# Conv states in three tiles and steps, first unit's weights split earlier, down steps in later slots of a two-layer trunk

## The chip, the cores and the metric

The kernel runs on one NeuronCore of a Trainium2 chip. The metric is the device time of one launch in microseconds. Each engine (TensorE = PE, VectorE = DVE, ScalarE = ACT, GpSimd = POOL, SyncE = SP) has its own instruction queue and works through it in order; one engine waits for another through semaphores only.

## What is computed

One inference step of a two-layer trunk for 512 prompt tokens and 8 samples of 8 tokens, 576 columns in all, with a model width of 1024. Layer 0 mixes with attention and a gated recurrence, layer 1 with a causal pooling; after each mixer follows the gated ConvFFN, which is where the change lies:

```python
def _conv_ffn(xn, prev, w_up, cw, cb, w_down):
    u = jnp.einsum("btd,df->btf", xn, w_up)            # 1024 -> 2 * 3072
    uc, new_prev = _causal_dwconv(u, prev, cw, cb)     # 3 taps; prev: state_ffn_conv of the samples
    g, val = jnp.split(uc, 2, axis=-1)
    return jnp.einsum("btf,fd->btd", jax.nn.gelu(g) * val, w_down), new_prev
```

## The kernel before

**Arithmetic.** Channels lie on the 128 partitions, tokens in the free dimension, in two halves of 288. Every operand of a matmul is split into a high and a low part (ACT rounds: "hi"; DVE subtracts: "lo"), and each product is three matmuls. So each weight block costs an ACT cast and a DVE subtraction (`wform`, lines 1375 and 1376, tiles `whl`), and each activation too (`hh`, `hl`, lines 1276 and 1277).

**The ConvFFN (`ffn`, line 1224 on).** The up projection makes 24 channel blocks of gate and value. The first six pairs go the usual way (`up_pair`, matmuls at line 143). The other 18 pairs go in 18 "units" (`unit`, line 1400): a unit n makes two channel blocks by seven products of 12 matmuls (line 1382), named "1" to "7", on sums and differences of weight quarters (made by POOL, lines 1407 to 1416) and of activations (`sums`, lines 1359 and 1360). Even n are gates, odd n values. At the end of a unit (`p3`) the two blocks go through the convolution (`conv`: POOL lines 1258 to 1260, ACT 1264, DVE 1265 and 1266); after an odd n comes the product of gate and value (`gate`: DVE 1272, 1273, then `hh`, `hl`).

**Down steps.** The down projection of four gated blocks (a group q) into output block m is a down step `(q, m)`: 24 matmuls (`dn_p`, line 1514) into two PSUM banks, one for each half of the columns. DVE then adds the two halves to the residual (`add_x`, line 711, "L711"), and that frees the banks. The pool of banks (tile `mmb`) has three, so the second bank of a down step is the one that the first L711 of the step ahead has freed, or the one of its second L711. The 32 down steps of q = 0 to 3 are put between other products: four in pairs 4 and 5, the other 28 in "slots" of the units: slot A lies between "6" (with "1" of unit n+1) and "7"; slot B lies after "7" and "2", "5" of unit n+1, and ahead of "4" and "3". `plan` (lines 1549 to 1575) lists the products in order. `prepare(j)` issues the weight splits of plan entry j, three entries ahead of its matmuls.

**What sets the order.** The program is written in the order of `plan`, but a scheduler at compile time places the instructions on each engine by their modelled readiness and by priority; `wform` and the evacuations of the products stand in high-priority blocks, the `gate` work and L711 do not. The finished order is fixed, and each engine runs its own part in order.

**Conv states.** The sample's states of the convolution (`state_ffn_conv`) come in 12 pieces (`states(a)`, line 1236): a DMA of 32 KB (line 1238, tile `fst`, two buffers), a PE transpose (line 1240), an ACT copy (line 1241). Two pieces are done in pair 0, the other ten one by one in later pairs as background steps (`self.bg`, run by `tick()`).

**Loads.** One SP queue issues all weight loads: raw weights of the pairs (`wraw`, line 120), quarters of the units (line 1394), down weights (`wd`, line 1504).

Of the kernel before, what the change touches and what calls it, by code (L numbers as in the profile page):

```python
# [8 lines left out]
F32 = mybir.dt.float32  # L9
# [34 lines left out]
class Trunk:  # L44
# [1179 lines left out]
    def ffn(self, l, after, first=0):  # L1224
# [8 lines left out]
        with self.tc.tile_pool(name="ff", bufs=2, reuse_waits="tile") as fp, ExitStack() as side:  # L1233
            stT = fp.tile([P, 48, 16], F32, name="fstT", bufs=1)

            def states(a):
                st = fp.tile([64, P], F32, name="fst", bufs=2)
                nc.sync.dma_start(st, so[:, a * 512:(a + 1) * 512].rearrange("r (j p) -> r j p", p=P))
                tp = self.bank()
                PE.transpose(tp[:, 0:64], st, self.ident[0:64, 0:64])  # L1240
                A.copy(stT[:, a * 4:(a + 1) * 4, :], tp[:, 0:64].rearrange("p (r j) -> p j r", j=4))

            for a in (1, 7, 2, 8, 3, 9, 4, 10, 5, 11):
                self.bg.append(lambda a=a: states(a))
            hs = {}
            uts = {}
            raws = {}
# [32 lines left out]
            def up_pair(i):  # L1280

                if i % 2 == 0:
                    for s in range(2):
                        if i == 0 and self.up0:
                            raws[s] = self.up0[0][s]
                            continue
                        raws[s] = self.raw(up[:, :, s * DFF + i * P:s * DFF + (i + 2) * P], 8, 256)
                pss = []
                for s in range(2):
                    if i == 0 and self.up0:  # L1290
                        hi, lo = self.up0[1][s]
                    else:
                        hi, lo = self.split(raws[s][:, :, i % 2 * P:i % 2 * P + P], 8, P)
                    pss.append(self.mm3(hi, lo, self.xs, 8, first, [self.px.tile([P, 512], F32, name="pu", tag="XY"[s], bufs=2)
                                                                   for _ in range(2)]))
                    if i == 0 and s == l:
                        states(0)
                        states(6)
                    if i:
                        for _ in range(2):  # L1300
                            if todo:
                                todo.popleft()()
                    if i >= 4:
                        down_now()
                if i == 5:
                    while todo:
                        todo.popleft()()
                    sums()
                ts = []
                for s in range(2):  # L1310
                    ps, u = pss[s], new_u(s, i)
                    V.tensor_tensor(u[:, 2:2 + HT], ps[0][:, 0:HT], self.rb[:, 0:HT], MUL)
                    V.tensor_tensor(u[:, 2 + HT:514], ps[1][:, 0:NP - HT], self.rb[:, HT:NP], MUL)
                    V.tensor_tensor(b10(u, 2, 8), b8(ps[1][:, NP - HT:HT]), b8(self.rb[:, NP:T]), MUL)
                    ts.append(conv(u, s, i))
                gate(i, *ts)
# [8 lines left out]
            def normed(fq):  # L1325
                for p in range(2):
                    xa.append(fq.tile([P, 4, HT], F32R, name="xa", tag=f"xa{p}", bufs=1))
                    xb.append(fq.tile([P, 4, T], F32R, name="xb", tag=f"xb{p}", bufs=1))
                for t, n in ((xa, "a0"), (xb, "b0")):
                    X[n] = [v[:, :, 0:HT] for v in t]  # L1330
                X["b1"] = [v[:, :, HT:T] for v in xb]

                def norm(c):
                    for k in (c, c + 4):
                        V.scalar_tensor_tensor(xn[k], self.xT[:, k, :], self.g_ffn(l, k), self.rb, MUL, MUL)

                def parts(c):
                    for x, v in ((xa, xn[c][:, 0:HT]), (xb, xn[c + 4])):
                        A.copy(x[0][:, c, :], v)
                        V.tensor_tensor(x[1][:, c, :], v, x[0][:, c, :].bitcast(F32), SUB)  # L1340

                def mixed(c):
                    a0, a1 = xn[c][:, 0:HT], xn[c][:, HT:T]
                    b0, b1 = xn[c + 4][:, 0:HT], xn[c + 4][:, HT:T]
                    V.tensor_tensor(a0, a1, a0, SUB)
                    V.tensor_tensor(a1, b1, a1, SUB)
                    V.tensor_tensor(b1, b1, a0, SUB)
                    V.tensor_tensor(b0, b0, b1, SUB)

                for c in range(4):  # L1350
                    for f in (norm, parts, mixed):
                        todo.append(lambda f=f, c=c: f(c))

            def sums():
                for h, (n0, n1) in enumerate((("t1", "t3"), ("t4", "t2"))):
                    th, tl = self.half("xh", h), self.half("xl", h)
                    for c in range(4):
                        v = xn[4 * h + c]
                        A.copy(th[:, c, :], v)
                        V.tensor_tensor(tl[:, c, :], v, th[:, c, :].bitcast(F32), SUB)  # L1360
                    X[n0] = [v[:, :, 0:HT] for v in (th, tl)]
                    X[n1] = [v[:, :, HT:T] for v in (th, tl)]

            box = deque()
            turn = [0]

            def wform(v):

# [18 lines left out]
            def load(n, f, h):  # L1387

                if n > 17:
                    return  # L1390
                if n < 2 and n not in rw:
                    rw[n] = self.wr.tile([P, 2048], F32, name="wraw", tag="wraw")
                c0 = n % 2 * DFF + (6 + n // 2 * 2 + f) * P
                nc.sync.dma_start(quarter(n, f, h), up[:, 4 * h:4 * h + 4, c0:c0 + P])
# [5 lines left out]
            def unit(n):  # L1400
# [80 lines left out]
                def p3(w):  # L1481
                    prod(st["Y"], w, X["b1"], False)
                    with self.tc.high_priority():
                        two(st["u"][0], st["Y"], st["c"])
                    ts[s] = [conv(st["u"][f], s, i + f) for f in range(2)]
                    if s:
                        for f in range(2):
                            gate(i + f, ts[0][f], ts[1][f])
                            if (i + f) % 4 == 3:

                                self.bg.extend([lambda: None] * 2)
                                for a in range(2):
                                    self.bg.append(lambda q=(i + f) // 4, a=a: tails(q, a))

# [25 lines left out]
            def tails(q, s):  # L1520
                tp = self.bank()
                PE.transpose(tp[0:72, 0:P], uts[q][:, s].rearrange("p r j -> p (r j)"), self.ident)
                tl = fp.tile([72, P], F32, name="tl", bufs=2)
                A.copy(tl, tp[0:72, 0:P])
                cs = slice(s * DFF + q * 512, s * DFF + (q + 1) * 512)
                nc.sync.dma_start(O["ffn_conv_p"][l, 0, :, cs].rearrange("b (j p) -> b j p", p=P), tl[0:8])
                nc.sync.dma_start(os_[:, cs].rearrange("b (j p) -> b j p", p=P), tl[8:72])
# [5 lines left out]
                dn_p(q, m, dn_w(q, m))  # L1533
                self.tick()

            self.psum(3)
            fq = side.enter_context(self.tc.tile_pool(name="fq", bufs=1, reuse_waits="tile"))
            for i in range(6):
                up_pair(i)
                if i == 0:  # L1540
                    normed(fq)
                if i == 3:
                    for s in range(2):
                        self.bg.append(lambda s=s: tails(0, s))
            for n in range(2):
                for f, h in ((0, 0), (1, 0), (1, 1), (0, 1)):
                    load(n, f, h)

            units = {}
            plan = []  # L1550

            def put(n, names):
                for c in names:
                    plan.append(("up", n, c))

            def put_down():
                plan.append(("down",) + downs.popleft())

            put(0, "12")
            put(1, "1")  # L1560
# [1 line left out]
            for n in range(18):  # L1562
                nx = n + 1 if n < 17 else None
                put(n, "6")
                if nx is not None and n:
                    put(nx, "1")
                if 1 <= n <= 10 or n in (12, 14):
                    put_down()
                put(n, "7")
                if nx is not None:  # L1570
                    put(nx, "25")
                if n < 16:
                    put_down()
                put(n, "43")
            assert not downs

            ready = {}

# [7 lines left out]
                    else:  # L1586
                        ready[j] = dn_w(a, b)

            for j in range(3):
                prepare(j)  # L1590
            for j, (kind, a, b) in enumerate(plan):
                prepare(j + 3)
                if kind == "up":
# [291 lines left out]
```

## Time and profile before

| | |
|---|---|
| time, median of 3 runs | 1267.13 us (1264.13 to 1269.37) |
| the profiled execution | 1277.01 us, its span 1275.3 us |
| PE busy | 1229.1 us, 96% of the span |
| DVE busy | 1001.1 us, 78% |
| ACT busy | 665.3 us, 52% |
| POOL busy | 432.9 us, 34% |

The profiled execution is 9.9 us above the median of the timed runs. PE is the engine to look at: in the 46.2 us in which it is idle another engine decides, and where its granted clock is below 1.00 its matmuls are slower. A row of a timeline gives start, duration, engine, line, operation, and in square brackets the idle time ahead of it on its engine with what ended it.

### The profile page before, as it was taken

Reading aid. Unit: us, or ns where it says so; the run is one execution under the profiler, and the core shown is the slowest. Engines: PE = TensorE matmul, PEld = TensorE weight load, DVE = VectorE, ACT = ScalarE, POOL = GpSimd, SP = SyncE. Lnnn points to the kernel's source line nnn. Section 1 sums busy time; section 2 is a strip of 40 time slices with the busy share of each in tenths; the row PEclk is TensorE's granted clock in tenths of the full one; section 3 lists DMA queues with packets and bytes.
Section 4 is the critical chain, followed back from the end, with each engine's and each line's share of the span. In section 5 each row is a group of like instructions: output and inputs, shape, how many; then the busy total and the mean of one; then the engine's idle time right before and its main releaser. Section 6 shows DMA issues by size and latency. Waiting matters only on the chain. (4 is left out here: it accounts for less than half of the span.)

```text
span 1275.3 us, 23464 instructions
## 1 busy us (share of the span) xinstructions
PE 1229.1 (96%) x8990; PEld 1170.4 (92%) x8990; DVE 1001.1 (78%) x1891; ACT 665.3 (52%) x1277; POOL 432.9 (34%) x674
## 2 busy tenths in 40 slices
PE   8989999999999899999999999999899999999998
PEld 6968887889899899999999999889899999999998
DVE  6827968897898788888878857798878988888941
ACT  6638557774445455455555535444454555555631
POOL 2240044410113444443544642211534434444400
PEclk9989999999999999999999999989999999999999
DMA  5314234323223223223321322322332323232231
GB/s 165 102 36 136 67 113 117 108 70 100 75 86 94 83 84 94 88 89 92 94 67 44 109 64 77 86 76 71 93 92 70 99 86 100 84 94 67 86 95 50
DMA packets 144772, 111.68 MB, mean 88 GB/s; under 512 B 8705, under 2 KB 135817, under 8 KB 144652
## 3 DMA queue, kind: packets, MB, share of 16 engines
q1 hardware_dynamic: 140516, 101.69, 26.1%
q0 software_dynamic: 3072, 8.46, 2.4%
q8 instruction: 71, 1.16, 0.4%
q14 instruction: 41, 0.34, 0.1%
q10 hardware_dynamic: 1072, 0.04, 0.1%
HBM read 104.14 MB, written 6.25 MB: 87 GB/s over the span
## 5 line engine op out<-in xcount | busy, mean ns | idle before, releaser
L1382 PE MATMUL pX<-xh,whl 128*128 128x288 f32 x864 | 192.4, 298 | 6.9 <-ACT c L1467 6.9
L1514 PE MATMUL mmb<-hh,whl 128*128 128x288 f32 x1024 | 190.0, 296 | 4.1 <-DVE xT L711 4.1
L1376 DVE TENSOR_TENSOR whl<-wraw,whl 128x512 fp32r<-128x512 f32 x216 | 155.8, 743 | 25.5 <-ACT whl L1375 23.9
L1514 PEld LDWEIGHTS mmb<-hh,whl 128*128 128x128 f32 x1024 | 154.6, 189 | 4.9 <-DVE xT L711 4.6
L1375 ACT CAST whl<-wraw 128x512 fp32r<-128x512 f32 x216 | 128.2, 620 | 47.5 <-PE mmb L1514 15.7
L1382 PEld LDWEIGHTS pX<-xh,whl 128*128 128x128 f32 x864 | 144.9, 188 | 8.1 <-ACT c L1467 7.4
L143 PE MATMUL pu<-xh,whl 128*128 128x288 f32 x768 | 143.1, 304 | 2.7 <-DVE whl L131 2.0
L1260 POOL COPY ut<-u 128x18 f32<-128x18 f32 x96 | 40.8, 425 | 279.0 <-DVE u L1444 164.7
L711 DVE TENSOR_TENSOR xT<-mmb,xT 128x288 f32<-128x288 f32 x174 | 72.3, 449 | 75.4 <-PE mmb L143 47.2
L1382 PE MATMUL pX<-xl,whl 128*128 128x288 f32 x432 | 127.7, 296 | 0.0
L130 ACT CAST whl<-wraw 128x1024 fp32r<-128x1024 f32 (+1 forms) x68 | 69.5, 1023 | 106.3 <-PE mmb L143 29.8
L143 PEld LDWEIGHTS pu<-xh,whl 128*128 128x128 f32 x768 | 116.7, 193 | 5.1 <-DVE whl L131 2.6
L1514 PE MATMUL mmb<-hl,whl 128*128 128x288 f32 x512 | 111.8, 298 | 5.5 <-DVE hl L1277 5.5
L1265 DVE SCALAR_TENSOR_TENSOR t<-u,par,t 128x592 f32<-128x592 f32 x96 | 96.3, 1007 | 23.7 <-ACT t L1264 23.4
L131 DVE TENSOR_TENSOR whl<-wraw,whl 128x1024 fp32r<-128x1024 f32 (+1 forms) x68 | 83.3, 1227 | 26.8 <-ACT whl L130 21.5
L1264 ACT ACTIVATE t<-u,par 128x592 f32<-128x592 f32 x96 | 84.3, 882 | 36.3 <-DVE u L1444 22.1
L1266 DVE SCALAR_TENSOR_TENSOR t<-u,par,t 128x592 f32<-128x592 f32 x96 | 90.5, 945 | 1.3
L1514 PEld LDWEIGHTS mmb<-hl,whl 128*128 128x128 f32 x512 | 82.7, 189 | 6.9 <-DVE hl L1277 6.9
L143 PE MATMUL pu<-xl,whl 128*128 128x288 f32 x384 | 84.8, 301 | 1.6 <-DVE xl L293 1.6
L1276 ACT CAST hh<-hf 128x576 fp32r<-128x576 f32 x48 | 32.4, 674 | 96.6 <-DVE hf L1273 95.8
L1382 PEld LDWEIGHTS pX<-xl,whl 128*128 128x128 f32 x432 | 81.4, 188 | 0.0
L1407 POOL TENSOR_TENSOR wraw<-wraw 128x512 f32<-128x512 f32 x36 | 58.4, 1623 | 46.4 <-DMA wraw<-in_ffn_w_up 39.8
(453 smaller groups left out, 3118.6 us busy)
## 6 DMA issues: line engine op xcount, KB each, us to landing
wraw<-in_ffn_w_up SPq DMA_DIRECT2D x144, 256.0 KB
wd<-in_ffn_w_down SPq DMA_DIRECT2D x32, 512.0 KB
wraw<-in_ffn_w_up SPq DMA_DIRECT2D x12, 1024.0 KB
wraw<-in_ab_w_in SPq DMA_DIRECT2D x9, 1024.0 KB
wraw<-in_ffn_w_down SPq DMA_DIRECT2D x8, 1024.0 KB
wraw<-in_ab_w_out SPq DMA_DIRECT2D x4, 1024.0 KB
xt<-in_x_prompt SPq DMA_DIRECT2D x4, 512.0 KB
out_y_p<-y SPq DMA_DIRECT2D x8, 256.0 KB
```

The source lines that it names most:

```text
L130: keep(self.nc.scalar.copy(hi, v))
L131: keep(self.nc.vector.tensor_tensor(lo, v, hi.bitcast(F32), SUB))
L143: nc.tensor.matmul(ps[hf][:, 0:HT], w[:, k, :], x[:, hf * HT:(hf + 1) * HT], start=(n == 0 and j == 0), stop=(n == K - 1 and j == 2))
L711: self.nc.vector.tensor_tensor(x, ps[hf][:, 0:HT], x, ADD)
L1264: A.activation(t, u[:, 2:594], AF.Identity, scale=self.fw(l, 2, ch), bias=self.fb(l, ch))
L1265: V.scalar_tensor_tensor(t, u[:, 1:593], self.fw(l, 1, ch), t, MUL, ADD)
L1266: V.scalar_tensor_tensor(t, u[:, 0:592], self.fw(l, 0, ch), t, MUL, ADD)
L1375: A.copy(f[:, 0], v)
L1376: V.tensor_tensor(f[:, 1], v, f[:, 0].bitcast(F32), SUB)
L1382: PE.matmul(ps[:, 0:HT], w[:, a, k, :], x[b][:, k, :], start=(start and k == 0 and j == 0), stop=(k == 3 and j == 2), skip_group_check=True)
L1407: G.tensor_tensor(a21, a11, a21, SUB)
L1514: PE.matmul(ps[hf][:, 0:HT], w[:, a, k, :], hs[4 * q + k][b][:, hf * HT:(hf + 1) * HT], start=(k == 0 and j == 0), stop=(k == 3 and j == 2))
```

## The change

Four edits in `ffn`, the same in both layers:

1. The 12 pieces of the conv states go into three tiles (in the buffers of the tag `hl`) by 12 DMAs at the entry of `ffn`; three steps of four transposes and four copies take the place of twelve steps. The first step runs in pair 0, the others as background steps.
2. The loads of units 0 and 1 and `prepare(0)`, `prepare(1)` move ahead of `sums()` in pair 5, `prepare(2)` behind it; the first `whl` buffer that `wform` takes is another (`turn`).
3. The list of slots: slot A before at n = 1 to 10, 12, 14, now at 1 to 14; slot B before at n = 0 to 15, now at 0 to 15 without 2 and 13. So the group q = 1 starts in slot A of n = 3 instead of slot B of n = 2, q = 2 in slot A of n = 7 instead of slot B of n = 6, q = 3 in slot A of n = 11 instead of slot B of n = 10.
4. `tails` (transposes of the new states, line 1522) come one tick later.

```diff
-            def states(a):
-                st = fp.tile([64, P], F32, name="fst", bufs=2)
-                nc.sync.dma_start(st, so[:, a * 512:(a + 1) * 512].rearrange("r (j p) -> r j p", p=P))
+            sts = []
+            for q in range(3):
+                t = fp.tile([P, T], F32, name="fst", tag="hl", bufs=9)
+                sts.append(t[0:64, 0:512].rearrange("p (a c) -> p a c", a=4))
+                for a in range(4):
+                    c0 = (a % 2 * 6 + 2 * q + a // 2) * 512
+                    nc.sync.dma_start(sts[q][:, a, :], so[:, c0:c0 + 512].rearrange("r (j p) -> r j p", p=P))
+
+            def states(q):
                 tp = self.bank()
-                PE.transpose(tp[:, 0:64], st, self.ident[0:64, 0:64])
...
-            for a in (1, 7, 2, 8, 3, 9, 4, 10, 5, 11):
-                self.bg.append(lambda a=a: states(a))
+                for a in range(4):
+                    PE.transpose(tp[:, a * 64:(a + 1) * 64], sts[q][:, a, :], self.ident[0:64, 0:64])
...
                     while todo:
                         todo.popleft()()
+                    for n in range(2):
+                        for f, h in ((0, 0), (1, 0), (1, 1), (0, 1)):
+                            load(n, f, h)
+                    prepare(0)
+                    prepare(1)
                     sums()
+                    prepare(2)
...
-            turn = [0]
+            turn = [2]
...
-                                self.bg.extend([lambda: None] * 2)
+                                self.bg.extend([lambda: None] * 3)
...
+            later = deque(list(downs)[4:])
...
-                if 1 <= n <= 10 or n in (12, 14):
+                if 1 <= n <= 14:
                     put_down()
                 put(n, "7")
                 if nx is not None:
                     put(nx, "25")
-                if n < 16:
+                if n not in (2, 15, 16, 17) and n != 13 or n == 15:
                     put_down()
                 put(n, "43")
```

The order on DVE in layer 0, unit 4, slot B, in the kernel before. Tiles carry their numbers: `mmb_5812` and `mmb_5813` are the two banks of the down step in slot A of the same unit, `hf`, `hl` belong to the gate of units 2 and 3, `c1` and `pZ` to the next unit's products, `whl_5882` to weights two products on.

```order
L1273 TENSOR_TENSOR hf_5760<-t_5531,t_5748 128x64
L1272 TENSOR_TENSOR hf_5768<-t_5538,t_5755 128x512
L1273 TENSOR_TENSOR hf_5768<-t_5538,t_5755 128x64
L711 TENSOR_TENSOR xT_73<-mmb_5812,xT_73 128x288
L1277 TENSOR_TENSOR hl_5764<-hf_5760,hh_5763 128x576
L1443 TENSOR_TENSOR u_5652<-pY_5659,c1_5857 128x224
L1444 TENSOR_TENSOR u_5652<-pY_5659,c1_5857 128x8x8
L1376 TENSOR_TENSOR whl_5882<-wraw_4863,whl_5882 128x512
L1376 TENSOR_TENSOR whl_5882<-d_5710,whl_5882 128x512
L1457 TENSOR_TENSOR u_5877<-pZ_5864,c1_5879 128x288
L1277 TENSOR_TENSOR hl_5772<-hf_5768,hh_5771 128x576
L711 TENSOR_TENSOR xT_73<-mmb_5813,xT_73 128x288
```

The same place now (layer 0, unit 4, slot B; lines are 15 higher except 711; `mmb_5752` and `mmb_5753` are the banks of the step in slot A):

```order
L1283 TENSOR_TENSOR hf_5699<-t_5483,t_5687 128x64
L1391 TENSOR_TENSOR whl_5804<-wraw_4795,whl_5804 128x512 x2
L1287 TENSOR_TENSOR hl_5703<-hf_5699,hh_5702 128x576
L1458 TENSOR_TENSOR u_5595<-pY_5603,c1_5800 128x224
L1459 TENSOR_TENSOR u_5595<-pY_5603,c1_5800 128x8x8
L1282 TENSOR_TENSOR hf_5707<-t_5490,t_5694 128x512
L1472 TENSOR_TENSOR u_5821<-pZ_5808,c1_5823 128x288
L1391 TENSOR_TENSOR whl_5842<-d_5647,whl_5842 128x512
L1391 TENSOR_TENSOR whl_5842<-wraw_4795,whl_5842 128x512
L1283 TENSOR_TENSOR hf_5707<-t_5490,t_5694 128x64
L711 TENSOR_TENSOR xT_73<-mmb_5752,xT_73 128x288
L711 TENSOR_TENSOR xT_73<-mmb_5753,xT_73 128x288
```

The first L711 of the step in slot A stood ahead of the evacuations (L1443, L1444, L1457) and of the four splits; now it stands behind them and behind the second L1283. The kernel before has such an order at one place in each layer, unit 12, slot B (`mmb_7508` and `mmb_7509` are the banks of the step in slot A of unit 12, layer 0):

```order
L1376 TENSOR_TENSOR whl_7554<-wraw_4863,whl_7554 128x512 x2
L1443 TENSOR_TENSOR u_7339<-pY_7347,c1_7550 128x224
L1444 TENSOR_TENSOR u_7339<-pY_7347,c1_7550 128x8x8
L1277 TENSOR_TENSOR hl_7453<-hf_7449,hh_7452 128x576
L1457 TENSOR_TENSOR u_7571<-pZ_7558,c1_7573 128x288
L1376 TENSOR_TENSOR whl_7592<-d_7397,whl_7592 128x512
L1376 TENSOR_TENSOR whl_7592<-wraw_4863,whl_7592 128x512
L1273 TENSOR_TENSOR hf_7457<-t_7265,t_7444 128x64
L711 TENSOR_TENSOR xT_73<-mmb_7508,xT_73 128x288
L711 TENSOR_TENSOR xT_73<-mmb_7509,xT_73 128x288
```

Now it has it at units 4, 6, 8, 10 and 12 of each layer, ten places in all; in each of them the tenth or eleventh matmul of slot B, the first one into the second bank, waits for the L711 of slot A.

The order of SP at the entry of `ffn`, layer 0, before:

```order
L1238 DMA fst<-in_state_ffn_conv 64x1x128 x2
L120 DMA wraw<-in_ffn_w_up 128x8x256
L1504 DMA wd<-in_ffn_w_down 128x4x256 x2
L120 DMA wraw<-in_ffn_w_up 128x8x256
L1238 DMA fst<-in_state_ffn_conv 64x1x128 x2
```

And now:

```order
L1243 DMA fst<-in_state_ffn_conv 64x1x128 x12
L120 DMA wraw<-in_ffn_w_up 128x8x256
L1519 DMA wd<-in_ffn_w_down 128x4x256 x3
L120 DMA wraw<-in_ffn_w_up 128x8x256 x5
L1409 DMA wraw<-in_ffn_w_up 128x4x128 x4
```

All twelve pieces stand ahead of the up weights of the later pairs; before, ten of them stood between and behind these.

## Rows read from the trace of the kernel before

**Rows 1.** The page's first part, busy time of each engine.
```profile
PE 1229.1 (96%) x8990; PEld 1170.4 (92%) x8990; DVE 1001.1 (78%) x1891; ACT 665.3 (52%) x1277; POOL 432.9 (34%) x674
```

**Rows 2.** PE's waits, grouped: line, releaser: us in total, times, longest us.
```profile
PE pX L1382 <- ACT c L1467: 6.9, 2, 3.4
PE mmb L1514 <- DVE hl L1277: 5.5, 6, 1.1
...
PE mmb L1514 <- DVE xT L711: 4.1, 2, 2.1
...
PE pu L143 <- DVE whl L131: 2.0, 3, 0.7
PE mmb L1522 <- DVE xT L711: 2.0, 2, 1.1
...
PE mmb L1240 <- ACT t L1270: 1.2, 1, 1.2
PE mmb L1240 <- DMA fst<-in_state_ffn_conv: 1.1, 3, 0.6
```

**Rows 3.** PE's timeline in unit 12, slot B, layer 0.
```profile
639.59 0.29 PE L1514 MATMUL mmb<-hh,whl 128*128 128x288 f32 x1
641.95 0.61 PE L1514 MATMUL mmb<-hh,whl 128*128 128x288 f32 x1 [2.06 <-DVE xT L711]
```

**Rows 4.** DVE's timeline there.
```profile
635.53 0.21 DVE L1273 TENSOR_TENSOR hf<-t 128x64 f32<-128x64 f32 x1
...
640.24 1.28 DVE L1273 TENSOR_TENSOR hf<-t 128x64 f32<-128x64 f32 x1
641.44 0.81 DVE L711 TENSOR_TENSOR xT<-mmb,xT 128x288 f32<-128x288 f32 x2
```

**Rows 5.** POOL's timeline there.
```profile
640.10 1.34 POOL L1409 TENSOR_TENSOR d<-wraw 128x512 f32<-128x512 f32 x1 [1.21 <-DMA wraw<-in_ffn_w_up]
```

**Rows 6.** PE's timeline in unit 12, slot B, layer 1.
```profile
1141.24 0.40 PE L1514 MATMUL mmb<-hh,whl 128*128 128x288 f32 x1 [2.06 <-DVE xT L711]
```

**Rows 7.** DVE's timeline in unit 8, slot B, layer 0.
```profile
568.98 0.22 DVE L1273 TENSOR_TENSOR hf<-t 128x64 f32<-128x64 f32 x1
569.12 0.45 DVE L711 TENSOR_TENSOR xT<-mmb,xT 128x288 f32<-128x288 f32 x1
```

**Rows 8.** Windows: stretch, length, PE busy (matmuls), granted clock, DMA share, GB/s.
```profile
420.00:425.00 5.00, 3.04 (x18) 0.85 0.36 104
425.00:430.00 5.00, 5.00 (x33) 0.81 0.18 53
625.00:650.00 25.00, 22.94 (x162) 0.93 0.27 78
840.00:845.00 5.00, 3.94 (x16) 0.50 0.09 23
845.00:850.00 5.00, 5.00 (x34) 0.83 0.00 0
...
1125.00:1150.00 25.00, 22.95 (x174) 1.00 0.26 77
```

**Rows 9.** SP's timeline at the entry of ffn, layer 1.
```profile
815.18 1.24 SPq L1238 DMA_DIRECT2D fst<-in_state_ffn_conv  x2
...
827.05 0.54 SPq L120 DMA_DIRECT2D wraw<-in_ffn_w_up  x1
```

**Rows 10.** PE's timeline at the first units, layer 0.
```profile
421.96 0.40 PE L1382 MATMUL pX<-xh,whl 128*128 128x288 f32 x1 [3.45 <-ACT c L1467]
```

**Rows 11.** POOL's timeline there.
```profile
412.93 2.96 POOL L1409 TENSOR_TENSOR d<-wraw 128x512 f32<-128x512 f32 x1 [5.95 <-issue]
415.96 1.61 POOL L1411 TENSOR_TENSOR wraw<-d,wraw 128x512 f32<-128x512 f32 x1
```

**Rows 12.** ACT's timeline there.
```profile
417.60 0.62 ACT L1375 CAST whl<-wraw 128x512 fp32r<-128x512 f32 x1 [3.73 <-POOL wraw L1411]
...
421.52 0.39 ACT L1467 COPY c<-pX 128x288 f32<-128x288 f32 x1
```

More of the change, by code (lines that the diff above doesn't have):

```diff
@@ L1234, in ffn @@
             stT = fp.tile([P, 48, 16], F32, name="fstT", bufs=1)
-            def states(a):
-                st = fp.tile([64, P], F32, name="fst", bufs=2)
-                nc.sync.dma_start(st, so[:, a * 512:(a + 1) * 512].rearrange("r (j p) -> r j p", p=P))
-                tp = self.bank()
-                PE.transpose(tp[:, 0:64], st, self.ident[0:64, 0:64])
-                A.copy(stT[:, a * 4:(a + 1) * 4, :], tp[:, 0:64].rearrange("p (r j) -> p j r", j=4))
-            for a in (1, 7, 2, 8, 3, 9, 4, 10, 5, 11):
-                self.bg.append(lambda a=a: states(a))
+            sts = []
[6 more added lines that the diff above has]
+            def states(q):
+                tp = self.bank()
+                for a in range(4):
+                    PE.transpose(tp[:, a * 64:(a + 1) * 64], sts[q][:, a, :], self.ident[0:64, 0:64])
+                for a in range(4):
+                    b = a % 2 * 6 + 2 * q + a // 2
+                    A.copy(stT[:, b * 4:(b + 1) * 4, :], tp[:, a * 64:(a + 1) * 64].rearrange("p (r j) -> p j r", j=4))
+            for q in (1, 2):
+                self.bg.append(lambda q=q: states(q))
             hs = {}
@@ L1297, in up_pair @@
                         states(0)
-                        states(6)
                     if i:
@@ L1534, in down_now @@
                 self.tick()
[L1536 to L1547, printed above, removed]
             units = {}
             plan = []
+            later = deque(list(downs)[4:])
             def put(n, names):
@@ L1556, in put_down @@
             def put_down():
-                plan.append(("down",) + downs.popleft())
+                plan.append(("down",) + later.popleft())
             put(0, "12")
@@ L1571, in ffn @@
                     put(nx, "25")
-                if n < 16:
+                if n not in (2, 15, 16, 17) and n != 13 or n == 15:
                     put_down()
                 put(n, "43")
-            assert not downs
+            assert not later
             ready = {}
@@ L1587, in prepare @@
                         ready[j] = dn_w(a, b)
-            for j in range(3):
-                prepare(j)
+            self.psum(3)
+            fq = side.enter_context(self.tc.tile_pool(name="fq", bufs=1, reuse_waits="tile"))
+            for i in range(6):
+                up_pair(i)
+                if i == 0:
+                    normed(fq)
+                if i == 3:
+                    for s in range(2):
+                        self.bg.append(lambda s=s: tails(0, s))
             for j, (kind, a, b) in enumerate(plan):
```

## The prediction

> **What bounds the kernel now.** I read the page's first part, then PE's waits, then PE's timeline around each long wait with the engines it waits for, and last the granted clock in windows. PE is busy for 1229.1 of 1275.3 us [rows 1], so PE's own work is fixed and only 46.2 us can be won from waits. The change adds and takes no matmul (28 down steps in the slots of each layer before and after, 12 transposes before and after), so its effect is a sum over PE's waits, and over the clock that PE loses behind them. The grouped waits show which ones it touches: six waits for `hl` of the gate at the first down step of a group (5.5 us), two for L711 (4.1), two at the first units for the copy `c` (6.9), the conv states' transposes (1.2 and 1.1), weights of the last pairs (2.0) and `tails` (2.0) [rows 2]. Together 22.8 us, and of these the change can win only a part.
>
> What a wait costs beyond its own length is in the windows. A window's loss is its length times one minus its granted clock. After the 3.45 us wait at 421.96 the two windows lost 0.75 and 0.95, together 1.70 us; around the states' transposes at 840 they lost 2.50 and 0.85, together 3.35 us; the 25 us that hold the 2.06 us wait of unit 12 lost 1.75 us in layer 0 and nothing in layer 1 [rows 8].
>
> **The slots.** Won: a group's first down step came in slot B right behind the gate that makes its `hl`; now it comes one product group later, in slot A of the next odd unit. In the changed order these steps wait for splits and banks only, whose releasers are done earlier. The six waits for `hl` go: -5.5 us [rows 2]. Nothing takes their place there that I can see.
>
> Lost: with three banks, a down step's second bank comes free only by an L711 of the step ahead. In the kernel before, at units 4 and 8 the first L711 of slot A stands right behind the gate's last product and runs at 569.12, long ahead of its use [rows 7]; PE has no wait there. At unit 12, slot B, the scheduler put both L711 behind two evacuations, four splits, `hl` and the second L1273, though their matmuls had ended long before. There DVE runs L1273 at 640.24, L711 at 641.44, and PE, which had started its last matmul into the first bank at 639.59, starts the next at 641.95 after 2.06 us of waiting [rows 3, 4]. Layer 1 has the same wait to the hundredth [rows 6]. The changed kernel's order has this sequence at units 4, 6, 8, 10 and 12 of both layers, ten places instead of two. DVE is behind from the gate on (it starts from the end of product "3", as PE does), so the length is set by the amount of work between the end of "3" and L711, which is the same set of instructions at all ten. I take 2.06 us for each: 20.6 us instead of 4.1, +16.5. With the -5.5 the slots cost +11.0 us.
>
> The size of a wait has two bounds. Part of the 2.06 us is a collision: L1273 took 1.28 us beside POOL's L1409 (1.34 us from 640.10), the same operation took 0.21 us five microseconds earlier [rows 4, 5]. Without the collision the wait is 2.06 - 1.07 = 0.99 us. With L711 where it stood at unit 8 it is zero [rows 7]. So the ten cost between 0 and 20.6 us; I take the upper end because L1409 is released by the split of `d` that DVE runs just ahead of L1273, and both stand in the same order now.
>
> The Trainium skill, "SBUF — State Buffer", section "Who interferes with whom", says that a DVE instruction with two SBUF inputs and a GpSimd instruction that reads SBUF exclude each other, and that whichever issues first keeps the shared ports for its whole length. The trace agrees: L1273 (two SBUF inputs) ends as L1409 does, and L711, which reads one input from PSUM, runs right behind. By that rule an L1409 that arrives 0.2 us later finds L1273 done, and the wait is the 0.99 us of the bound above.
>
> **The clock behind these waits.** One of two such waits cost 1.75 us of clock, the other none [rows 8]. For ten I take half: 8.75 us, less the 1.75 that is there now: +7.0, bounds -1.75 and +15.75.
>
> **The conv states.** In layer 1 three transposes waited for their DMA or for a bank still held by an ACT copy, 2.3 us together with layer 0's, and the clock lost 3.35 us behind them [rows 2, 8]. Now all pieces are requested at the entry, so the last two steps can't meet a late DMA. The 12 DMAs take 12 x 0.62 = 7.4 us of SP, from 815.2 to about 822.6, and the up weights of the next pair were issued only at 827.05 [rows 9], so nothing is queued behind them that is needed. The work of PE and ACT (12 transposes and copies) is the same. Worth: -2.3 - 3.35 = -5.65; if the conv of pair 0 now ends later (four transposes and four copies stand ahead of it instead of two), up to 1 us of this comes back, and the clock may fall anyway: bounds -5.65 and 0. I take -5.65.
>
> **The first units.** PE's 3.45 us wait in layer 0 (6.9 us in both) [rows 2, 10] is the end of a chain: POOL's L1409 takes 2.96 us beside two `xl` subtractions on DVE, L1411 1.61 us [rows 11]; the cast of its result runs at 417.60 on ACT, idle 3.73 us before it, and the copy `c` stands behind it in ACT's queue, at 421.52 [rows 12]. The change puts unit 1's first split ahead of part of the `sums`. It does not take POOL's two operations out of the chain: in the changed order the fourth `xl` stands on DVE behind splits whose cast waits for that same L1411, so the wait moves to product "5" of unit 0. If only the collision goes, L1409 takes 1.34 instead of 2.96 us [rows 5, 11], and 1.62 of 3.45 is won. Bounds: nothing, and 3.45 each. I take 1.62 twice: -3.2, and the clock's 1.70 us for one of the two layers: -1.7 (bounds 0 and -3.4). The splits of unit 0's products, now in a buffer that the last up pair's matmuls must release, still come ahead of their use, since the last down step of pair 5 lies between; if they did not, an ACT cast of 0.62 us and the split behind it would show as a new wait ahead of unit 0.
>
> **The rest.** The three waits for weights of the last pairs (2.0 us) fall next to POOL work that moves; I take -0.7, bounds -2.0 and 0. The `tails` come one tick later: they still wait for a bank behind L711 (2.0 us) [rows 2], 0, bounds ±2.
>
> **The sum.** 11.0 + 7.0 - 5.65 - 3.2 - 1.7 - 0.7 = +6.7 us. It is made against the profiled execution (1277.01 us: 1275.3 of span and 1.7 around it), which would become 1283.7. The timed runs lie 9.9 us lower; I carry the difference over unscaled: 1267.13 + 6.7 = 1273.8, about 1274 us. A difference under 0.5% (6.3 us) can't be told from no change here, so the forecast lies just on the slow side of that bound.
>
> **Rivals.**
> - *The late L711 don't cost.* Place: slot B of units 4 to 12. L1409 asks after L1273 instead of before, so each wait is 0.99 us: 9.9 us, against 9.6 (5.5 and 4.1) taken away, +0.3. Waits of that length cost no clock (the six for `hl` show no low window that I found), so the 1.75 goes as well. With the other gains: 0.3 - 1.75 - 5.65 - 3.2 - 1.7 - 0.7 = -12.7, so 1254 us. It decides from a wait of about 1.6 us per place downward, where the ten cost 6.4 more than the 9.6 taken away, which the states pay for. For it speaks that POOL's unit work did not collide at unit 8's L1273 (0.22 us) [rows 7]; against it that both layers show 2.06 [rows 3, 6]. Chance 0.25.
> - *The waits recur, the clock stays.* 11.0 - 1.75 - 11.25 = -2.0, so 1265 us. For it: layer 1's window at 1.00. Chance 0.22.
> - *The clock falls behind nearly every wait.* +8.75 more than in the forecast: 6.7 + 8.75 = +15.5, 1282.6 us. For it: layer 0's window, and both windows after the wait at 421.96 [rows 8]. Chance 0.13.
> - The change doesn't do what it says: the `hl` waits would stay in slot A of n = 3, 7 and 11. Their gate is more than a unit back by then, so I give this no chance of its own.
>
> The forecast itself (ten waits near 2 us, half of them with a fall of the clock) has 0.40, and a range of 1267 to 1281. Faster by over 0.5%: the first rival and a tenth of the second, with part of larger gains at the first units: 0.28. Within 0.5%: most of the second, and the third or so of the forecast that ends below 1273.4: 0.30. Slower: 0.42. For 8 in 10 the range reaches from the first rival's centre to the last one's: 1254 to 1283.
>
> **What would show it.** Right: PE's waits at L1529 for L711 appear ten times or so with about 2 us each, those for `hl` (L1287) are gone, L1283 takes 1.3 us beside POOL's L1424 ahead of each, and no L1248 waits for `fst`. Wrong: the L711 waits at L1529 together stay under 10 us, or the granted clock in the units falls in none of the windows that hold them. The first units are wrong if no wait of 1 to 2.5 us stands between products "2" and "7" of unit 0.

## The result and the profile after

The changed kernel takes 1286.77 us (median of 4 runs, 1282.77 to 1286.99) against 1266.16 us before: ratio 1.0142, 95% interval [1.0123, 1.0162], so 18.0 us slower by the ratio and 20.6 by the medians. I forecast 1274, a slowdown of 6.7 us: the right side, under half of the size, and above the range. The profiled execution (1286.78 us) lies at the median.

PE's waits, grouped, in the changed kernel (line, releaser: us in total, times, longest), to be held against [rows 2]:

```profile
PE mmb L1529 <- DVE xT L711: 20.6, 10, 2.2
PE pY L1397 <- DVE xl L1375: 5.6, 2, 4.6
PE pu L143 <- DVE whl L131: 4.8, 3, 1.9
...
PE pX L1397 <- DVE xl L1375: 3.4, 1, 3.4
PE mmb L143 <- DVE xT L711: 3.2, 2, 2.2
```

The first row is the forecast one: ten waits for L711 and 20.6 us, the very sum of the prediction (the single waits are 1.98 to 2.23 us). No wait for `hl`, none for `fst` and none for the `tails` is left. But the other rows are no gains: the first units wait 9.0 us for `xl` where they waited 6.9 for `c`, and the weights of the pairs (L131) cost 4.8 instead of 2.0.

One of the ten places, layer 0, unit 8, first PE's, then DVE's, then POOL's timeline (as [rows 3 to 5]):

```profile
566.54 0.29 PE L1529 MATMUL mmb<-hh,whl 128*128 128x288 f32 x1
568.82 0.40 PE L1529 MATMUL mmb<-hh,whl 128*128 128x288 f32 x1 [1.98 <-DVE xT L711]
```

```profile
566.51 0.68 DVE L1391 TENSOR_TENSOR whl<-wraw,whl 128x512 fp32r<-128x512 f32 x1
567.11 1.28 DVE L1283 TENSOR_TENSOR hf<-t 128x64 f32<-128x64 f32 x1
568.32 0.81 DVE L711 TENSOR_TENSOR xT<-mmb,xT 128x288 f32<-128x288 f32 x2
```

```profile
566.72 1.59 POOL L1424 TENSOR_TENSOR d<-wraw 128x512 f32<-128x512 f32 x1 [1.03 <-DVE whl L1391]
```

L1283 takes 1.28 us beside L1424, and L711 runs right behind it, as the kernel before did it once per layer.

Windows in the changed kernel (stretch, length, PE busy, granted clock, DMA share, GB/s): the first units of layer 0, layer 0's five places, and the first units of layer 1:

```profile
410.00:415.00 5.00, 1.90 (x8) 0.58 0.19 56
415.00:420.00 5.00, 5.00 (x30) 0.74 0.18 52
475.00:500.00 25.00, 22.77 (x161) 0.93 0.24 70
525.00:550.00 25.00, 22.96 (x173) 1.00 0.29 86
550.00:575.00 25.00, 23.02 (x175) 1.00 0.26 77
600.00:625.00 25.00, 22.96 (x174) 1.00 0.29 85
625.00:650.00 25.00, 23.00 (x175) 1.00 0.26 77
...
920.00:925.00 5.00, 1.81 (x6) 0.78 0.18 53
925.00:930.00 5.00, 4.78 (x21) 0.54 0.18 52
```

In this execution the clock fell behind one of the ten waits, by 1.75 us: the windows of layer 1's five places read 1.00 too. At the first units it lost 3.4 us in each layer. Over all runs the mean granted clock is 0.9916 in 25 runs of the kernel before (10.6 us lost of 1266) and 0.9878 in the four of the changed one (15.7 us of 1284).

### The profile page after: what moved, and what is told of

Same layout as the page of the kernel before. It is cut to its first block, busy times and chain, and to the rows that moved or that the text cites. A ratio compares the mean times of both kernels' runs of the same rounds, so it can differ in the third digit from the quotient of the medians.

```text
span 1285.1 us, 23455 instructions
## 1 busy us (share of the span) xinstructions
PE 1228.4 (96%) x8990; PEld 1172.7 (91%) x8990; DVE 1020.9 (79%) x1891; ACT 667.2 (52%) x1277; POOL 452.4 (35%) x674
## 5 line engine op out<-in xcount | busy, mean ns | idle before, releaser
L1529 PE MATMUL mmb<-hh,whl 128*128 128x288 f32 x1024 | 194.4, 297 | 20.6 <-DVE xT L711 20.6
L1391 DVE TENSOR_TENSOR whl<-wraw,whl 128x512 fp32r<-128x512 f32 x216 | 162.2, 771 | 27.5 <-ACT whl L1390 25.1
L1270 POOL COPY ut<-u 128x18 f32<-128x18 f32 x96 | 51.8, 540 | 312.1 <-DVE u L1459 203.7
L711 DVE TENSOR_TENSOR xT<-mmb,xT 128x288 f32<-128x288 f32 x174 | 71.6, 448 | 66.0 <-PE mmb L143 49.9
L1529 PE MATMUL mmb<-hl,whl 128*128 128x288 f32 x512 | 115.1, 297 | 0.0
L131 DVE TENSOR_TENSOR whl<-wraw,whl 128x1024 fp32r<-128x1024 f32 (+1 forms) x68 | 82.7, 1217 | 20.5 <-ACT whl L130 20.1
L143 PE MATMUL mmb<-hh,whl 128*128 128x288 f32 x384 | 69.5, 297 | 3.2 <-DVE xT L711 3.2
L1431 POOL TENSOR_TENSOR wraw<-wraw,d 128x512 f32<-128x512 f32 x36 | 57.0, 1583 | 44.1 <-DVE whl L1391 44.1
```

Of the source, the lines that this page charges most:

```text
L131: keep(self.nc.vector.tensor_tensor(lo, v, hi.bitcast(F32), SUB))
L143: nc.tensor.matmul(ps[hf][:, 0:HT], w[:, k, :], x[:, hf * HT:(hf + 1) * HT], start=(n == 0 and j == 0), stop=(n == K - 1 and j == 2))
L711: self.nc.vector.tensor_tensor(x, ps[hf][:, 0:HT], x, ADD)
L1391: V.tensor_tensor(f[:, 1], v, f[:, 0].bitcast(F32), SUB)
L1431: G.tensor_tensor(a12, a12, st["d"], SUB)
L1529: PE.matmul(ps[hf][:, 0:HT], w[:, a, k, :], hs[4 * q + k][b][:, hf * HT:(hf + 1) * HT], start=(k == 0 and j == 0), stop=(k == 3 and j == 2))
```

## The experiments

Each was timed beside the kernel before in the same job; "before" in a row is that median. "Changed" is the changed kernel.

**The kernel before again.** 

> The kernel before, unchanged, for a second trace of it. Theory: the first profiled execution held a loss at 84 us (4.83 us of waiting for ACT at L1774 and a clock of 0.6 to 0.7 for 10 us, about 8 us together) that the timed runs do not have; without it this trace reads about 1268 us, with the same waits as before in the two ConvFFNs. Rival: the wait at L1774 is there again, and the 9.9 us between profile and median lie elsewhere (clock in the ConvFFNs).

Measured: 1267.46 us (before 1267.84), ratio 0.9993 [0.9975, 1.0011]; its profiled execution 1262.72 us, PE busy 1220.3 of 1261.0 us. The wait at L1774 is not there, and the windows that lost 3.45 us behind it in the first trace read 1.00. In the first trace:

```profile
83.89 0.62 PE L1774 MATMUL mmb<-xch,wb 128*128 128x300 f32 x1 [4.83 <-ACT a__257 L1777]
```

So some 8 us of that trace were of that one execution. The waits in the ConvFFNs are nearly the same (`c` 6.9, `hl` 5.4, L711 4.1, the states' transposes 2.3, now all of them for `fst`); PE's idle time that the changed kernel has to be held against is 40.7 us, not 46.2. This trace in its turn lies 4.7 us under the median of its runs. The low clock at the first units costs 1.7 us in each layer here; layer 0's windows:

```profile
410.00:415.00 5.00, 2.82 (x12) 0.70 0.36 103
415.00:420.00 5.00, 5.00 (x38) 0.96 0.18 54
```

**The new slots alone**, on the kernel before:

```diff
-                if 1 <= n <= 10 or n in (12, 14):
+                if 1 <= n <= 14:
...
-                if n < 16:
+                if n not in (2, 15, 16, 17) and n != 13 or n == 15:
```

> The kernel before with the new list of slots alone (edit 3 alone). Theory: ten waits of 2.06 us for L711 against 9.6 us taken away, 11 us slower than before, about 1277 us. Rival (clock): 15 us slower or more. Rival (entry and first units): under 6 us slower.

Measured: 1284.77 us (before 1267.84), ratio 1.0130 [1.0099, 1.0162], +17 us. PE's waits for L711:

```profile
PE mmb L1514 <- DVE xT L711: 19.2, 10, 2.1
```

And three windows of this execution in which one of the ten waits lies or has just ended:

```profile
530.00:535.00 5.00, 4.67 (x23) 0.66 0.00 0
605.00:610.00 5.00, 3.33 (x14) 0.66 0.00 0
...
1040.00:1045.00 5.00, 5.00 (x28) 0.66 0.00 0
```

19.2 us of waits against 9.5 taken away is +9.7; the mean clock of its four runs is 0.9853, 18.9 us lost instead of 10.6, +8.3. The two together are 18.0 where 16.9 were measured. The clock rival holds here: nearly half of what the slots cost alone is clock, about as the prediction had put it (11.0 and 7.0). In this trace 5.1 us of it stand behind three of the ten waits. Two of the ten, at unit 4 of each layer, are only 1.31 and 1.37 us long: in layer 1 L1409 starts at 1001.94, behind L1273 (1001.73, 0.22 us) and with L711 (1001.86), so it does not hold L1273 up.

**The old slots in the changed kernel** (the same lines undone). 

> The changed kernel with the old list of slots (edit 3 undone, edits 1, 2 and 4 kept). Theory (late L711): the ten waits of 20.6 us become two of 4.1, the six waits for hl (5.5) come back, so 11 us faster than the changed kernel, about 1276 us; 9 us stay, which are the other edits' and the clock's. Rival (clock): the clock falls behind the ten waits in most runs, then undoing the slots gives 15 us or more, 1271 or less. Rival (entry and first units): the slots carry little, under 6 us, 1281 or more.

Measured: 1271.22 us (before 1267.84), ratio 1.0028 [1.0007, 1.0048]: 15.5 us under the changed kernel by the medians, 14.5 by the ratios, on the border of what the clock rival asks. But here it is the waits and not the clock: `hl` 6.2 and L711 1.9 us are 8.1 instead of 20.6, 12.5 less, and the mean clock of the ten runs is 0.9896 (13.2 us lost instead of 15.7), 2.5 less. What is left of the change, edits 1, 2 and 4, is 3.4 us slower than before (0.9 to 6.1).

The two waits for L711 at unit 12, 2.06 us each in the kernel before, are 0.93 us here. In layer 0, PE, DVE and POOL:

```profile
630.98 0.41 PE L1529 MATMUL mmb<-hh,whl 128*128 128x288 f32 x1 [0.93 <-DVE xT L711]
```

```profile
630.34 0.22 DVE L1283 TENSOR_TENSOR hf<-t 128x64 f32<-128x64 f32 x1
630.47 0.81 DVE L711 TENSOR_TENSOR xT<-mmb,xT 128x288 f32<-128x288 f32 x2
```

```profile
631.93 1.29 POOL L1424 TENSOR_TENSOR d<-wraw 128x512 f32<-128x512 f32 x1 [2.94 <-DMA wraw<-in_ffn_w_up]
```

POOL's operation waits for its DMA and starts after both; L1283 takes 0.22 us, and the wait is near the 0.99 us that the prediction gave for a wait without the collision. The windows from 625 to 640 and, for layer 1, from 1125 to 1140 read a clock of 1.00.

**L711 with high priority**, in the changed kernel:

```diff
                 if k == 3:
-                    self.add_x(m, ps)
+                    with self.tc.high_priority():
+                        self.add_x(m, ps)
```

> The changed kernel with the add of a down step to the residual (L711) issued with high priority, all else kept; in the order L711 then stands ahead of the gate's work at the ten places. Theory: the ten waits go whole, 20.6 us, about 1266 us. Rival: DVE has no slack there, and what L711 now overtakes is late instead (PE waits for a split or an evacuation), so less than 10 us come back, 1277 or more.

Measured: 1268.16 us (before 1267.84), ratio 1.0001 [0.9978, 1.0023]; 18.6 us under the changed kernel by the medians, 17.9 by the ratios. No wait for L711 is left in the units. DVE's timeline in this kernel, in a unit that waited before:

```profile
555.76 0.81 DVE L711 TENSOR_TENSOR xT<-mmb,xT 128x288 f32<-128x288 f32 x2
556.50 1.27 DVE L1391 TENSOR_TENSOR whl<-wraw,whl 128x512 fp32r<-128x512 f32 x2
...
558.13 0.21 DVE L1283 TENSOR_TENSOR hf<-t 128x64 f32<-128x64 f32 x1
```

The two L711 take 0.74 us ahead of the splits; what they delay there shows on PE as 0.28 us once in each layer. It was the order, not a lack of time on DVE. PE's waits show what stands against the 20.6 us: 1.75 us for `c` near the end of each layer's units, which the changed kernel did not have, and 11.4 us instead of 9.0 for `xl`. And the clock did not come back: the mean of the ten runs is 0.9860 (17.7 us lost), no higher than the changed kernel's 0.9878 (15.7). So most of the changed kernel's low clock does not hang on the ten waits.

**New slots and early L711 on the kernel before** (the two diffs above). 

> The kernel before with the new slots and with L711 of a down step issued with high priority. Theory: neither the six waits for hl (5.4 us) nor the two for L711 (4.1) nor the ten of the new slots are left: 9.5 us faster than before, about 1258 us. Rival (DVE has no slack): evacuations or splits are late in their place, 1264 or more.

Measured: 1259.53 us (before 1267.98), ratio 0.9927 [0.9900, 0.9953], 8.5 us faster: the later slots do win the `hl` waits, once L711 is not late. Here the clock does come back: 12.8 us are lost by the mean of the runs, 18.9 with the new slots alone.

**The state tiles alone** (edit 1 on the kernel before). 

> The kernel before with the three state tiles alone (edit 1 alone). Theory (DVE late at the entry): the waits for fst go (2.3 us), but the splits of the next pairs' weights come late behind DVE's normalisation work, as in the changed kernel (waits for L131 4.8 us instead of 2.1), so it is 0 to 3 us slower than before. Rival, as predicted: 2 to 5.7 us faster.

Measured: 1274.50 us (before 1267.98), ratio 1.0062 [1.0036, 1.0088], +6.5 us, worse than either expected. The waits for `fst` are gone, but the pairs' weights come late:

```profile
PE pu L143 <- DVE whl L131: 8.9, 5, 3.8
```

Where it begins, in layer 1: ACT, DVE and PE of this kernel.

```profile
819.98 0.56 ACT L1250 COPY fstT<-mmb 128x64 f32<-128x64 f32 x4 [2.46 <-PE mmb L1247]
```

```profile
815.59 0.21 DVE L1322 TENSOR_TENSOR u<-pu,rb 128x64 f32<-128x64 f32 x1
...
821.40 1.61 DVE L1274 SCALAR_TENSOR_TENSOR t<-u,par,t 128x592 f32<-128x592 f32 x2 [2.62 <-ACT t L1273]
...
841.09 1.22 DVE L131 TENSOR_TENSOR whl<-wraw,whl 128x1024 fp32r<-128x1024 f32 x1
```

```profile
842.36 0.85 PE L143 MATMUL pu<-xh,whl 128*128 128x288 f32 x2 [3.84 <-DVE whl L131]
```

And the kernel before (its second trace), DVE at the same conv:

```profile
807.78 0.21 DVE L1314 TENSOR_TENSOR u<-pu,rb 128x64 f32<-128x64 f32 x1
...
812.14 0.83 DVE L1265 SCALAR_TENSOR_TENSOR t<-u,par,t 128x592 f32<-128x592 f32 x1 [1.18 <-ACT t L1264]
```

With four transposes in a lump the first conv of pair 0 starts on DVE 5.8 us after its `u` (815.59 to 821.40), before it was 4.4 (807.78 to 812.14). After one more pause of 0.96 us DVE is busy for the whole of 826.4 to 842.3, and the split of a later pair is the one that is late.

**Eight empty background steps behind the state steps** (so that the first `tails` are not pulled forward by the eight steps that are gone):

```diff
             for q in (1, 2):
                 self.bg.append(lambda q=q: states(q))
+            self.bg.extend([lambda: None] * 8)
```

> The kernel before with the three state tiles (edit 1 alone) and eight empty background steps behind them, so that the first group's tails keep the place they had behind ten state steps. Theory (tails too early): of the 6.5 us that edit 1 costs, the early tails carry the waits for POOL's ut and ACT's tl (1.2 us in layer 0) and part of the late splits of pair 5 (2.1 us there), so the time falls to 2 to 4 us above the kernel before. Rival (late conv of pair 0 and its splits): the waits for L131 stay at 8 us or more, and the time at 5 us or more above.

Measured: 1273.58 us (before 1269.90), ratio 1.0030 [1.0016, 1.0045], +3.7 us. The waits for POOL's `ut` and for `tl` are gone, L131 is at 6.3 us instead of 8.9. So the early tails may carry up to half of edit 1's cost; it is not shown, since the interval overlaps that of edit 1 alone and the medians differ by 0.9 us. The 3.84 us in layer 1 stay.

**The first state step behind the gate's matmuls in both layers** (`s == l` becomes `s == 0`). 

> The kernel before with the three state tiles (edit 1 alone), but with the first step put behind pair 0's gate matmuls in both layers (layer 1 had it behind the value matmuls too). Theory (late conv of pair 0): in edit 1 the conv of pair 0 begins about 1.5 us later, since four transposes come as one lump behind the matmuls, and DVE never makes that up before the splits of pairs 1 to 4 are due; with the lump earlier in layer 1 its waits for L131 (3.8 and 1.1 us there) shrink by at least 2 us, and the time falls from 6.5 to 2 to 4 us above the kernel before. Rival (DMA): the transposes now wait for fst on PE, and as much is lost there; the time stays 6 us above.

Measured: 1275.96 us (before 1268.65), ratio 1.0053 [1.0033, 1.0073], +7.3 us. In layer 1 the 3.84 us wait for L131 fell to 0.83, but 1.11 us of waiting for `u`, 2.04 for pair 5's split and 1.2 for the tails stand there now. The price moved; the total stayed, and the theory that the late lump alone is the cost fell.

**The first units' earlier splits alone** (edits 2 and 4 on the kernel before). 

> The kernel before with the earlier weight splits of the first units alone (edits 2 and 4). Theory (xl behind splits): in both layers the wait for c (6.9 us) becomes waits for xl in product 5, 8 to 10 us, and the clock falls as far, so 1 to 4 us slower than before. Rival, as predicted: 3 to 5 us faster, since only the wait of POOL's L1409 beside DVE goes.

Measured: 1270.06 us (before 1267.98), ratio 1.0024 [1.0008, 1.0040], +2.1 us. The 6.9 us for `c` became 9.5 for `xl` and 1.1 for `c`. In the changed kernel the place in layer 0 reads, PE, DVE, POOL and ACT (as [rows 10 to 12]):

```profile
413.10 0.61 PE L1397 MATMUL pY<-xl,whl 128*128 128x288 f32 x1 [4.57 <-DVE xl L1375]
```

```profile
408.11 3.20 DVE L1391 TENSOR_TENSOR whl<-wraw,whl 128x512 fp32r<-128x512 f32 x2
411.24 1.81 DVE L1375 TENSOR_TENSOR xl<-xn,xh 128x576 fp32r<-128x576 f32 x1
```

```profile
407.28 1.67 POOL L1426 TENSOR_TENSOR wraw<-d,wraw 128x512 f32<-128x512 f32 x1
...
410.73 1.70 POOL L1431 TENSOR_TENSOR wraw<-wraw,d 128x512 f32<-128x512 f32 x1
```

```profile
408.98 0.62 ACT L1390 CAST whl<-wraw 128x512 fp32r<-128x512 f32 x1 [3.46 <-POOL wraw L1426]
```

The last `xl` stands behind two splits, of which the second waits for the cast that waits for L1426; the chain of the kernel before has only changed the instruction that PE stands at. In layer 1 the waits at this place are 3.37 us for `xl` and 0.56 for `c`.

**The splits of `sums` with high priority** in the changed kernel. 

> The changed kernel with the splits of sums (xh, xl) issued with high priority, so that the fourth xl of each half stands ahead of the splits of unit 1 on DVE. Theory (xl behind splits): of the 9.0 us of waits for xl at the first units at least 5 go, and a part of the clock with them: 5 to 8 us faster than the changed kernel, 1279 to 1282 us. Rival: the wait moves to the split or to c behind L1426 of POOL, as it was before the change, under 3 us faster.

Measured: 1285.63 us (before 1267.98), ratio 1.0128 [1.0085, 1.0170], 1 us under the changed kernel. The rival holds: the waits for `xl` are gone, and PE waits 5.5 us for `c` (3.8 of them in layer 0) and 3.6 us for splits instead.

**Two buffers for `d`** in the changed kernel (odd units the old one, even units another). 

> The changed kernel with a second buffer for the difference d (POOL's L1424), odd units in the old one and even units in a new one. Theory (POOL waits for the split of d): at the first units L1424 of unit 1 no longer waits until DVE has split unit 0's d, POOL runs about 5 us earlier, and the 9.0 us of waits for xl there fall under 4 us; beside that L1283 no longer meets L1424 in the units, so that the ten L711 waits are 1.0 us each instead of 2.06: 10 us. Together 13 to 17 us faster than the changed kernel, 1270 to 1274 us. Rival (DVE's load alone): the collision only moves to another DVE operation, both waits stay within 20%.

Measured: 1287.96 us (before 1268.65), ratio 1.0155 [1.0136, 1.0174], no gain. PE's waits:

```profile
PE mmb L1529 <- DVE xT L711: 20.8, 10, 2.2
PE pu L143 <- DVE whl L131: 7.0, 4, 2.0
...
PE pY L1397 <- DVE xl L1375: 3.2, 2, 1.7
...
PE pX L1397 <- DVE whl L1391: 2.3, 2, 1.2
```

At the first units the waits for `xl` fell from 9.0 to 4.8 us, so POOL did wait for the split of `d`; other waits took most of it. In the units the rival holds. POOL's and DVE's timelines of this kernel at unit 8, slot B:

```profile
563.25 1.71 POOL L1424 TENSOR_TENSOR d<-wraw 128x512 f32<-128x512 f32 x1 [0.33 <-DMA wraw<-in_ffn_w_up]
```

```profile
563.73 1.78 DVE L1391 TENSOR_TENSOR whl<-wraw,whl 128x512 fp32r<-128x512 f32 x1
565.43 0.21 DVE L1283 TENSOR_TENSOR hf<-t 128x64 f32<-128x64 f32 x1
565.57 0.81 DVE L711 TENSOR_TENSOR xT<-mmb,xT 128x288 f32<-128x288 f32 x2
```

POOL's operation comes earlier and blocks the split ahead of L1283 instead: the same microsecond, one instruction sooner.

**New slots, early state step, two buffers for `d`, late L711.** 

> The kernel before with the new slots, the state tiles with the early first step, and two buffers for d. Theory (POOL waits for the split of d): the wait for c at the first units (6.9 us) falls under 3 us, the ten L711 waits are about 1.0 us each. Rival (DVE's load alone): both as long as in the new slots alone, 6.9 and 19 us.

Measured: 1288.91 us (before 1268.65), ratio 1.0147 [1.0124, 1.0170]. `c` 3.7 us instead of 6.9 (above the 3 expected), L711 23.6 us instead of 19.2: the second `d` does not shorten these waits.

**All together:** new slots, early L711, two `d`, early state step. 

> The new slots, L711 with high priority, two buffers for d, and the state tiles with the early first step, on the first units of the kernel before. Theory: no wait for L711 or hl in the units, the wait for c under 3 us: at least as fast as the new slots with the early L711 (1259.5 us), 1254 to 1260. Rival: the states' lump costs what two buffers win, 1260 to 1264.

Measured: 1259.36 us (before 1268.65), ratio 0.9926 [0.9910, 0.9942]: no better than slots and L711 alone (0.9927). With the eight empty steps: 

> All of the combined kernel (new slots, early L711, two buffers for d, early states) with the eight empty background steps. Theory (tails too early): 2 to 4 us under the combined kernel, 1255 to 1257 us. Rival: no change, 1259 us.

Measured: 1257.65 us (before 1269.90), ratio 0.9898 [0.9882, 0.9915]: 1.7 us better by the medians, 3.5 by the ratios, and the two intervals just touch.

**The old states in the changed kernel.** 

> The changed kernel with the conv states as before (edit 1 undone). Theory (edits add): edit 1 costs about 4 to 6.5 us in the changed kernel as it does alone, so 1280 to 1283 us. Rival (edits hide one another): beside edit 2 the first units wait anyway for what the late splits delay, so undoing edit 1 gives less than 3 us, 1284 or more.

Measured: 1283.61 us (before 1269.90), ratio 1.0136 [1.0093, 1.0179]; the interval covers the changed kernel's ratio of 1.0142. Whether edit 1 costs as much beside the others as alone is left undecided. Its waits are plain, though: without edit 1 PE waits 0.7 us for L131 instead of 4.8, and 1.3 us for `fst` again.

**The best: new slots, early L711, two buffers for `d`, states as before** (the tile `tl` shares the buffers of `fst`):

```diff
-self.res.tile([P, T], F32, name="d", tag="sqacc", bufs=1)[:, 0:512]
+(self.res.tile([P, T], F32, name="d", tag="sqacc", bufs=1)[:, 0:512] if n % 2
+ else fp.tile([P, 512], F32, name="d", tag="dd", bufs=1))
```

> The new slots, early L711 and two buffers for d, with the conv states as before (tl shares the two buffers of fst to make room). Theory: the wait for c at the first units falls from 6.9 to under 4 us and nothing of edit 1 is paid: 1254 to 1257 us. Rival: the shared buffer or POOL beside the splits of the last pair costs as much, 1259 us.

Measured: 1255.30 us (before 1269.90), ratio 0.9886 [0.9870, 0.9903], the fastest here, within the theory's range. Its waits:

```profile
PE pX L1382 <- ACT c L1467: 4.7, 4, 2.4
...
PE pY L1382 <- DVE u L1444: 2.5, 2, 1.2
PE mmb L1240 <- DMA fst<-in_state_ffn_conv: 2.4, 4, 1.1
```

The wait for `c` is above the 4 us expected, and 2.5 us for `u` are new: PE is idle for 32.3 us, no less than in the kernel with new slots and early L711 alone (31.1). The gain over that kernel is in the clock (6.6 us lost by the mean of the runs instead of 12.8), and their intervals touch. That the second `d` is its cause is not shown.

## Why the prediction was wrong

- *The slots, +11.0 us of waits:* right, in mechanism and size. Ten waits, 20.6 us, `hl` gone; alone 9.7 us, and the early L711 gives 18.6 us back.
- *The clock behind them, +7.0:* about right for the slots alone, where 8.3 us more were lost and the early L711 gave 6.1 back. In the changed kernel it is too much: the trace has 1.75 us behind one of the ten waits, and the clock is no higher with the waits gone. The whole clock still costs 5.1 us more than before (15.7 against 10.6) where the sum had +2.0 (7.0 less 3.35 and 1.7). That the +2.0 lies on the side of these 5.1 is luck: they come for the most part from other places than the ten waits.
- *The conv states, -5.65:* this step failed. I took the waits for `fst` and the low clock behind them as won, since "the work of PE and ACT is the same". The waits went, but the work moved: the first conv is later, the tails come earlier, and L131 is late instead (4.8 us in the changed kernel, 0.7 with the old states in it). Alone the edit costs 6.5 us. I had bounded it at zero. How the 6.5 us divide between the late conv and the early tails stays open.
- *The first units, -3.2 and -1.7:* this step failed too. I saw where the wait would move to, and then priced it by one POOL operation. It is 9.0 us for `xl` and 0.6 for `c` instead of 6.9 for `c`: in layer 0 the last `xl` stands behind two splits, the second of them waits for POOL's L1426, and `xl` itself takes 1.81 us beside L1431. The clock, which I had as a gain of 1.7, lost 3.4 us at this place in each layer where the second trace of the kernel before lost 1.7. Alone edits 2 and 4 cost 2.1 us.
- *The rest, -0.7:* the waits for L131 in the changed kernel went up by 2.8 us, which belongs to the states. The 2.0 us of the `tails`, priced at 0, are gone.

In sum, PE's idle time rose from 40.7 us (second trace) to 56.7: 11.1 of these 16.0 us are the slots, as forecast, and 4.9 are the other waits, where the sum had -6.2. With the 5.1 us of clock that is 21.1 us, an estimate from one trace of each kernel and the mean clock of their runs; the medians differ by 20.6. The edits alone cost 17, 6.5 and 2.1 us, by the ratios 2.2% together where the change as a whole costs 1.4%, so their prices do not simply add.

The rival of short waits (0.99 us each) was open: with the old slots both waits at unit 12 were 0.93 us, and with the new slots alone unit 4's were 1.31 and 1.37, since POOL's operation came after L1273 (now L1283). In the changed kernel it came beside it, as I had assumed; that all ten did was not certain from the order.

## What to carry to other kernels

Price a removed wait only up to the next one in the same chain: if the engine behind it works without a pause (here DVE, 15.9 us on end), what is moved ahead makes something else late, and zero is no bound on the side of the loss. Look in the new order for the instruction that frees a buffer (here L711, 0.4 us long): where the scheduler lets it fall behind long work, it sets the pace, and here raising its priority took back 18.6 us. And look at a second trace before taking one trace's waits as the kernel's.

## What the hardware showed

A wait of 2 us in a stretch of full PE work cost about 1.7 us of clock or nothing: in the trace of the changed kernel behind one of ten, in that of the new slots alone behind three of ten (1.70 us each, a mean granted clock of 0.66 for 5 us). Behind the two waits of 0.93 us the clock stayed at 1.00. Over runs: mean clock 0.9916 in the kernel before (0.9904 in the job of the best kernel), 0.9853 with the new slots alone, 0.9948 in the best kernel.

DVE and POOL hold one another up. With the second `d` POOL's operation was released by its DMA instead of DVE's split, and the DVE operation that it met took 1.78 us instead of 0.68. This agrees with the Trainium skill, "SBUF — State Buffer", section "Who interferes with whom": a DVE instruction with two SBUF inputs and a GpSimd instruction that reads SBUF contend, and issue order decides who blocks. What that costs PE hangs on the place: with POOL's operation ahead of L711, beside the split or beside L1283, PE's wait was about 2 us; with POOL's operation after L711 it was 0.93 us, and with the two starting together 1.31 and 1.37.
